# Moving weights and operands by bytes within their buffers: split weights 192 bytes on in place of 64, one block operand 112 bytes on

## The chip, the cores and the metric

The kernel runs on one core of one Trainium2 chip. The metric is the device time of one execution in microseconds. The kernel before takes 1206.85 us (median of three runs, 1206.4 to 1207.08).

## What is computed

A two-layer decoder trunk on 512 tokens of width 1024, all in float32: RMSNorm, a token mixer, a residual add, RMSNorm, a SwiGLU FFN, a residual add; then the second layer and a last RMSNorm. The first layer's mixer is dilated window attention in three groups of eight heads, the second layer's a causal pooling mixer.

```python
def reference(x, attn_norm, w_qkv, w_attn_out, pool_norm, w_pool_in, w_pool_group, pool_scale,
              ffn_norm, w_ffn_gate_up, w_ffn_down, final_norm):
    for i in range(DEPTH):
        j = i // N_MIXERS
        if i % N_MIXERS == 0:
            x = x + dilated_attention_mixer(rmsnorm(x, attn_norm[j]), w_qkv[j], w_attn_out[j])
        else:
            x = x + pooling_mixer(rmsnorm(x, pool_norm[j]), w_pool_in[j], w_pool_group[j], pool_scale[j])
        x = x + swiglu_ffn(rmsnorm(x, ffn_norm[i]), w_ffn_gate_up[i], w_ffn_down[i])
    return rmsnorm(x, final_norm)
```

## The kernel before

Tokens lie along the free axis (512 columns), channels on the 128 partitions. Every large product is made exactly enough in float32 by splitting each operand into a high part, rounded to the matmul's input type, and a low part, the rest: a product is then three matmuls, high x high, high x low and low x high. These three are lines 424, 425 and 426 in `mult`, lines 294, 295 and 297 in `Product.add`, and lines 595, 596 and 597 in `values12`.

*Two kinds of product.* `Product` takes a plain unit of weights (class `Plain`): an 8 x 8 block product with 512 columns streamed in each matmul. `mult` serves `seven` and `chained`, which make two blocks of output from seven products of half size (Strassen's scheme, as Winograd arranges it), each with 256 columns streamed. Their weights come in a `Pair`: blocks, sums, more sums and the last block, which `Pair.steps` lists and `take` splits. Attention uses `seven` for queries, keys and the first group's values; the FFN uses `chained` for gate/up and for some of the down products. `values12` makes the other values of attention with the roles swapped: there the weights are streamed and the token operand is loaded.

*Stages.* In the traced execution attention with `seven` runs from about 100 to 425 us, the first FFN to about 806 us, the pooling mixer to about 870 us, the second FFN after that, and the last rows of output from about 1180 us. An FFN is cut into parts by `PARTS`; a part whose third entry is true makes its down products by `chained` on the hidden units as blocks (`operands`, `operands_right`, `operands_left` place them under keys `d`). They run from about 655 to 694 us and from 1015 to 1055 us, and for the first layer also around 770 to 800 us. The last two of the eight output blocks of the second layer are computed in halves of 256 columns with plain weights (`end`, at the bottom of the kernel), so that the last norm can begin early.

*Where operands lie.* Three kinds of buffers matter.
- Split weights: the rings `w` (five buffers) and `half` (two). A buffer has room for a high and a low part and `LINE` = 64 elements (256 bytes) more; class `Held` places both parts `shift` elements on (an element is 4 bytes). `Plain` asks for no shift. `pairs` passes its `shift` to `Pair`: 16 elements by default, which attention's queries, keys and first values take, `APART` = 28 elements for the pairs of `values12`, and 0 for all of the FFN.
- Split token operands: two big tiles, `near` (11 places) and `far` (15 places), each with some room behind, handed out by `slot`. With `apart=True` an operand is placed `APART` = 28 elements (112 bytes) on; the FFN's block operands are, attention's are not.
- Two more places outside the big tiles, the loose ones (`slot11` and `slot12`), which `slot` gives when the big tiles have no place. They are tiles of their own and have no shift, whatever `apart` says.

All these buffers begin at 128 modulo 256 bytes in their partition, so the offsets that the code adds decide how operand and weights stand to each other modulo 256 bytes.

*Order.* Nothing is scheduled automatically: the engines take their instructions in the order in which the program issues them. Weights are loaded ahead by `pump`, which runs after each block of a product: it issues the next load as soon as its buffers are free and then the next split. A load of a `Pair` is three DMAs from SP's queue and one from POOL's, which adds to data in place (line 160). The program reserves `dynamic_dma_scratch_size` bytes of each partition for the descriptors of POOL's DMAs.

Of the kernel before, what the change touches and what calls it, by code (L numbers as in the profile page):

```python
# [15 lines left out]
P = 128  # L16
S = 512
D = 1024
KC = D // P
HEADS = 8  # L20
DFF = 2816
FC = DFF // P
# [22 lines left out]
BUFS = {"w": 5, "half": 2, "raw": 4, "rawhalf": 2}  # L45
COLS = {"w": D, "half": D // 2, "raw": D, "rawhalf": D // 2}
LINE = 64
APART = 28
NEAR = 11
OPEN = 2  # L50
# [4 lines left out]
def units_of(n):  # L55
    return (n,) if n <= KC else (n // 2, n - n // 2)
# [7 lines left out]
def trunk(ctx: ExitStack, tc: tile.TileContext, xT, norms, w_first, w_qk, w_qkp, w_v0, w_v0p, w_v12, w_out, w_pair, w_down, w_dblock, w_pin, w_pgrp,  # L64
          consts, ident_in, invcnt_in, outT, outR):
    nc = tc.nc
    cpool = ctx.enter_context(tc.tile_pool(name="cpool", bufs=1))
# [23 lines left out]
    def split(hi, lo, v):  # L91
        nc.scalar.activation(hi, v, AF.Copy)  # L92
        nc.vector.tensor_tensor(lo, v, hi.bitcast(F32), op=OP.subtract)  # L93
# [7 lines left out]
    class Held:  # L101


        def __init__(self, ring, shift=0):
            self.live = True
            n = COLS[ring]
            if ring in ("w", "half"):
                t = wpool.tile([P, 2 * n + LINE], F32R, tag=ring, name=ring, bufs=BUFS[ring])
                self.t = [t[:, shift + i * n:shift + (i + 1) * n] for i in range(2)]
            else:  # L110
                self.t = wpool.tile([P, n], F32, tag=ring, name=ring, bufs=BUFS[ring])
            rings[ring].append(self)
# [8 lines left out]
    class Plain:  # L121


        def __init__(self, *srcs):
            self.srcs, self.n, self.w = srcs, sum(src.shape[-1] for src in srcs), None
            loads.append((self, {"raw": 1}, self.load))
            steps.append((self, "w", self.split))

# [5 lines left out]
                o += src.shape[-1]  # L134

        def split(self):
            self.w = Held("w")
            split(*(t[:, :self.n] for t in self.w.t), self.raw.t[:, :self.n])
            self.raw.done()

    class Pair:
# [21 lines left out]
        def take(self, name, ring, raw):  # L163
            self.w[name] = w = Held(ring, self.shift)
            w.n = self.n
            split(*(t[:, :raw.shape[-1]] for t in w.t), raw)
# [20 lines left out]
    loads, steps, units = deque(), deque(), deque()  # L187
# [15 lines left out]
                return  # L203
            steps.popleft()[2]()

    def pairs(*srcs, shift=LINE // 4, back=False):

        these = [Pair(src, shift, back) for src in srcs]
        for parts in zip(*(p.steps() for p in these)):
            steps.extend(parts)  # L210
        units.append(these)

    def plain_gu(layer, j):
        src = w_pair[layer, j]
        units.extend([Plain(src[:, S:3 * S]), Plain(src[:, 3 * S:], src[:, :S])])

    def plain(*srcs):
        units.extend([Plain(src) for src in srcs])

    for h in range(HEADS):  # L220
        if h == 0:
            plain(*[w_qk[u] for u in range(len(QK) - NF)])
        for g in range(3):
            if h == 1 and g < NSOLO:
                plain(*[w_qk[len(QK) - NF + 2 * g + c] for c in range(2)])
            elif h:
                pairs(w_qkp[3 * h - 3 - NSOLO + g])
        if h == 0:
            plain(w_v0[0], w_v0[1])
        elif h % 2 == 0:  # L230
            pairs(w_v0p[h // 2 - 1])
        else:
            pairs(w_v12[h // 2, 0], w_v12[h // 2, 1], shift=APART)
    plain(*[w_out[m] for m in range(KC)])

    def ffn_plan(layer):
        j = 0
        for i, (first, end, block) in enumerate(PARTS[layer]):
            while j < min(end + block, FC):
                if j < NPLAIN:  # L240
                    plain_gu(layer, j)
                else:
                    pairs(w_pair[layer, j], shift=0, back=True)
                j += 1
            if block:
                for m in range(K2):
                    pairs(w_dblock[sum(p[2] for l in range(layer) for p in PARTS[l]) + sum(p[2] for p in PARTS[layer][:i]), m],
                          shift=0, back=True)
            else:
                for m in range(KC):  # L250
                    o = first * P
                    for n in units_of(end - first):
                        units.append(Plain(w_down[layer, m, :, o:o + n * P]))
                        o += n * P

    ffn_plan(0)
    plain(*[w_pin[m] for m in PIN_ORDER])
    ffn_plan(1)

    def weights():  # L260
# [5 lines left out]
    class Product:  # L266
# [16 lines left out]
        def add(self, ks, cols=slice(0, S), pos=None):  # L283
            for k in ks:
                if self.w:
                    w, c = self.w, k if pos is None else pos + k
                else:
                    held, c = self.where(k)
                    w = held.t
                    if c == self.sizes[len(self.tiles) - 1] - 1 and not self.keep:  # L290
                        held.done()
                s = slice(c * P, (c + 1) * P)
                mh, ml = self.ins(k)
                nc.tensor.matmul(self.p[:, cols], w[0][:, s], mh[:, cols], start=self.done == 0, stop=False)  # L294
                nc.tensor.matmul(self.p[:, cols], w[0][:, s], ml[:, cols], start=False, stop=False)  # L295
                self.done += 1
                nc.tensor.matmul(self.p[:, cols], w[1][:, s], mh[:, cols], start=False, stop=self.done == self.n)  # L297
            if not self.w:
                pump(2)
            return self  # L300
# [4 lines left out]
    def slot(name, dtype=F32R, apart=False, open=False, far=False):  # L305


        top, low = range(FIXED + SLOTS - 1, FIXED - 1, -1), range(FIXED, FIXED + SLOTS)
        near, loose = list(range(NEAR)), list(range(NEAR, FIXED))
        if "far" not in room:  # L310
            top = low = []
        if dtype == F32 or open:
            order = loose
        elif apart:
            order = [*top, *near[::-1], *loose]
        else:
            order = [*low, *near, *loose] if far else [*near, *low, *loose]
        i = next(i for i in order if i not in taken and (i in loose or taken.get(i + 1) is not False if apart else i in loose or not taken.get(i - 1)))
        if i in loose:
            taken[i] = None  # L320
            return i, cpool.tile([P, 2, S], dtype, tag=f"slot{i}", name=name, bufs=1)
        taken[i] = apart
        o = (i - FIXED * (i >= FIXED)) * 2 * S + APART * apart
        return i, room["far" if i >= FIXED else "near"][:, o:o + 2 * S].rearrange("p (e c) -> p e c", e=2)

    room["near"] = cpool.tile([P, NEAR * 2 * S + LINE], F32R, name="near")

# [10 lines left out]
    def product(layer):  # L338
        return Product(KC, stream(layer)).add(range(KC)).p
# [20 lines left out]
    def note(layer, k):  # L360

        if layer < 4:
            held[layer, k], t = slot("h", open=layer == 2 and k == KC - 1)
            scaled(layer, k, t[:, 0], t[:, 1])
        square(layer, k)
# [163 lines left out]
    class Temp:  # L529
        def __init__(self):  # L530
            self.i, t = slot("temp", F32)
            self.t = t.rearrange("p e c -> p (e c)")
# [30 lines left out]
    with tc.tile_pool(name="opool", bufs=1) as opool:  # L563
        early = opool.tile([P, HEADS, S], F32R, tag="o", name="early")
        with tc.tile_pool(name="apool", bufs=1) as apool:
# [253 lines left out]
            H, T, o = {}, {}, []  # L819
# [92 lines left out]
            for c in range(2):  # L912
                p = product(0)
# [57 lines left out]
            for m in range(KC):  # L971
                if lead:
                    f = lead.pop(0).add([last])
                else:
                    f = Product(HEADS, heads).add(range(HEADS))
# [6 lines left out]
    with tc.tile_pool(name="fpool", bufs=2) as fpool:  # L982

        room["far"] = fpool.tile([P, SLOTS * 2 * S + LINE // 2], F32R, tag="far", name="far", bufs=1)

# [284 lines left out]
        def end(i, half, js, f=None):  # L1270
            f = f or Product(HALF, hidden, keep=ends[i])
            return f.add(js, cols=halves[half])
# [39 lines left out]
        def total(half, sq):  # L1312
            t = ftile("total", H2)
            nc.vector.tensor_add(t, acc[4][:, halves[half]], sq)
            return t

        t = total(0, add(0, 0, end(0, 0, range(HALF))))
        sq = add(1, 0, end(1, 0, range(HALF)))
        f = end(0, 1, range(5))
        r = rstd([t, sq])  # L1320
        end(0, 1, range(5, HALF), f)
        t = total(1, add(0, 1, f))
        f = end(1, 1, range(1))
# [3 lines left out]
        f = end(1, 1, range(1, HALF), f)  # L1327
# [96 lines left out]
```

## Time and profile before

| | |
|---|---|
| median of three runs | 1206.85 us (1206.4 to 1207.08) |
| profiled execution, its own time | 1206.44 us |
| its span, first to last instruction | 1204.6 us |
| granted TensorE clock, mean | 0.998 |
| busy: PE, weight loads (PEld), DVE, ACT, POOL | 1193.7, 1117.6, 966.3, 658.0, 138.7 us |
| DMA | 183.65 MB, mean 152 GB/s |

PE is the matmul engine, PEld its weight loads, which overlap the matmuls. In the groups by line a row gives the line, engine, operation, tile written <- tiles read, shape and count, then busy time in us and the mean duration of one in ns, then the engine's idle time before them. Matmuls are pipelined: a clean one of 256 columns shows 275 ns, though the next begins some 113 ns after it. A longer duration goes with a later start of the next. In a table of stretches a row has start and end, length, busy time with the count of instructions, the granted clock, the share of time in which the DMA engines are busy, and GB/s.

### The profile page before, as it was taken

How to read it: one execution, taken by the hardware profiler on the slowest of the kernel's cores; microseconds unless marked ns; L12 is line 12 of the kernel's file. 1: busy time of each engine (PE TensorE's matmuls, PEld its weight loads, DVE VectorE, ACT ScalarE, POOL GpSimd, SP SyncE). 2: the span in 40 equal slices, each digit the busy share in tenths (PEclk: the TensorE clock that was granted, in tenths of full speed). 3: DMA queues.
4: the chain of work that ended last, by engine and by line, in shares of the span. 5: the costliest groups of instructions: out<-in, count | busy, mean ns of one | idle time of the engine just before them, and what ended most of it. 6: DMA issues, size and time to landing. Idle time of an engine off the chain costs nothing.

```text
span 1204.6 us, 24247 instructions
## 1 busy us (share of the span) xinstructions
PE 1193.7 (99%) x9720; PEld 1117.6 (93%) x9720; DVE 966.3 (80%) x1650; ACT 658.0 (55%) x1162; POOL 138.7 (12%) x131
## 2 busy tenths in 40 slices
PE   9999999999999999999999999999999999999997
PEld 7889999999999988888999999988788999999987
DVE  7888888878889854965898889989997898788633
ACT  6545554555556543542677567663443676566531
POOL 1111111111111100101111111000300111111000
PEclk9999999999999999999999999999999999999999
DMA  8346667666756532336677777644016677777322
GB/s 292 112 103 171 144 158 169 162 166 150 179 150 158 190 123 91 96 106 142 177 199 192 186 196 192 182 149 140 28 53 166 162 196 187 192 192 190 110 77 71
DMA packets 71152, 183.65 MB, mean 152 GB/s; under 512 B 7152, under 2 KB 8320, under 8 KB 71040
## 3 DMA queue, kind: packets, MB, share of 16 engines
q1 hardware_dynamic: 49824, 140.41, 35.7%
q0 software_dynamic: 21072, 41.43, 20.9%
q8 instruction: 76, 1.25, 0.4%
q14 instruction: 36, 0.29, 0.1%
q10 hardware_dynamic: 144, 0.26, 0.1%
HBM read 179.98 MB, written 2.10 MB: 151 GB/s over the span
## 4 chain that ended last, share of the span: by engine, by line
PE 91%; DVE 5%; issue 2%; ACT 1%; POOL 0%; DVEq 0%; POOLq 0%; DMA 0%; ACTq 0%
PE ps L424 17%; PE ps L425 17%; PE ps L426 17%; PE ps L294 9%; PE ps L295 9%; PE ps L297 9%; PE ps L595 2%; PE ps L597 2%; PE ps L596 2%; DVE w L93 1%; PE ps L807 1%; PE ps L679 1%; DVE s L1223 1%; PE ps L699 1%; PE ps L801 1%
## 5 line engine op out<-in xcount | busy, mean ns | idle before, releaser
L92 ACT ACTIVATE w<-raw 128x1024 fp32r<-128x1024 f32 (+3 forms) x303 | 309.8, 1028 | 258.3 <-PE ps L297 84.3
L93 DVE TENSOR_TENSOR w<-raw,w 128x1024 fp32r<-128x1024 f32 (+3 forms) x303 | 356.1, 1180 | 76.3 <-ACT w L92 72.3
L424 PE MATMUL ps<-far,w 128*128 128x256 f32 x860 | 236.7, 275 | 0.0
L425 PE MATMUL ps<-far,w 128*128 128x256 f32 x860 | 236.7, 275 | 0.0
L426 PE MATMUL ps<-far,w 128*128 128x256 f32 x860 | 236.6, 275 | 0.0
L425 PEld LDWEIGHTS ps<-far,w 128*128 128x128 f32 x860 | 161.5, 188 | 0.1
L424 PEld LDWEIGHTS ps<-far,w 128*128 128x128 f32 x860 | 161.5, 188 | 0.1
L426 PEld LDWEIGHTS ps<-far,w 128*128 128x128 f32 x860 | 161.4, 188 | 0.0
L424 PE MATMUL ps<-near,w 128*128 128x256 f32 x556 | 158.1, 284 | 1.5 <-ACT first L506 1.5
L425 PE MATMUL ps<-near,w 128*128 128x256 f32 x556 | 154.3, 278 | 0.0
L426 PE MATMUL ps<-near,w 128*128 128x256 f32 x556 | 154.3, 277 | 0.0
L295 PE MATMUL ps<-near,w 128*128 128x512 f32 (+1 forms) x364 | 137.7, 378 | 0.6 <-DVE near L357 0.6
L294 PE MATMUL ps<-near,w 128*128 128x512 f32 (+1 forms) x364 | 138.1, 380 | 0.0
L297 PE MATMUL ps<-near,w 128*128 128x512 f32 (+1 forms) x364 | 137.3, 378 | 0.0
L424 PEld LDWEIGHTS ps<-near,w 128*128 128x128 f32 x556 | 104.8, 188 | 2.5 <-ACT first L506 2.1
L425 PEld LDWEIGHTS ps<-near,w 128*128 128x128 f32 x556 | 104.6, 188 | 0.0
L426 PEld LDWEIGHTS ps<-near,w 128*128 128x128 f32 x556 | 104.5, 188 | 0.0
L160 POOL DMA_DIRECT2D raw<-w_pair x34 | 41.2, 1210 | 366.5 <-DMA raw<-w_pair 200.1
L295 PEld LDWEIGHTS ps<-near,w 128*128 128x128 f32 x364 | 68.5, 188 | 14.0 <-DVE near L357 1.7
L297 PEld LDWEIGHTS ps<-near,w 128*128 128x128 f32 x364 | 68.5, 188 | 12.8
L294 PEld LDWEIGHTS ps<-near,w 128*128 128x128 f32 x364 | 68.5, 188 | 12.5
L92 ACT ACTIVATE half<-rawhalf 128x512 fp32r<-128x512 f32 x75 | 47.2, 631 | 14.4 <-PE ps L426 12.3
(323 smaller groups left out, 2671.1 us busy)
## 6 DMA issues: line engine op xcount, KB each, us to landing
raw<-w_pair SPq DMA_DIRECT2D x78, 512.0 KB, 4.5
raw<-w_qkp SPq DMA_DIRECT2D x36, 512.0 KB, 4.2
raw<-w_pair POOLq DMA_DIRECT2D x34, 512.0 KB, 7.4
raw<-w_dblock SPq DMA_DIRECT2D x24, 512.0 KB, 4.1
raw<-w_v SPq DMA_DIRECT2D x18, 512.0 KB, 4.4
raw<-w_qkp POOLq DMA_DIRECT2D x18, 512.0 KB, 7.6
rawhalf<-w_pair SPq DMA_DIRECT2D x34, 256.0 KB, 5.1
raw<-w_dblock POOLq DMA_DIRECT2D x12, 512.0 KB, 7.5
```

Source lines behind the costliest of these rows:

```text
L92: nc.scalar.activation(hi, v, AF.Copy)
L93: nc.vector.tensor_tensor(lo, v, hi.bitcast(F32), op=OP.subtract)
L160: nc.gpsimd.dma_start(self.b.rearrange("p (a c) -> p a c", a=2), self.src[:, None, 3 * n:].to_broadcast([P, 2, n]), accum_op=OP.add)
L294: nc.tensor.matmul(self.p[:, cols], w[0][:, s], mh[:, cols], start=self.done == 0, stop=False)
L295: nc.tensor.matmul(self.p[:, cols], w[0][:, s], ml[:, cols], start=False, stop=False)
L297: nc.tensor.matmul(self.p[:, cols], w[1][:, s], mh[:, cols], start=False, stop=self.done == self.n)
L424: nc.tensor.matmul(dst, w.t[0][:, c], th, start=k == 0 and not on, stop=False, skip_group_check=on)
L425: nc.tensor.matmul(dst, w.t[0][:, c], tl, start=False, stop=False, skip_group_check=on)
L426: nc.tensor.matmul(dst, w.t[1][:, c], th, start=False, stop=k == n - 1, skip_group_check=on)
L595: nc.tensor.matmul(o, mh, wh, start=k == 0, stop=False)
L596: nc.tensor.matmul(o, mh, wl, start=False, stop=False)
L597: nc.tensor.matmul(o, ml, wh, start=False, stop=k == K2 - 1)
```

## The change

Only addresses change; what is computed, loaded and issued, and in which order, stays.
- The default shift of `pairs` goes from 16 to 48 elements, that is from 64 to 192 bytes. `values12` and the FFN pass their own and keep it.
- The plain weights of the last two output blocks of the second layer's last FFN part get a shift of 48 elements in place of 0.
- The two loose tiles become 256 bytes larger, and with `apart=True` their operand lies 28 elements (112 bytes) on, as in the big tiles.
- To make room, POOL's descriptor scratch goes from 4096 to 2048 bytes a partition. The tiles ahead of the loose ones move down by 2048 bytes and those behind by 1536, both multiples of 256.

```diff
+BEHIND = 48
...
-        def __init__(self, *srcs):
-            self.srcs, self.n, self.w = srcs, sum(src.shape[-1] for src in srcs), None
+        def __init__(self, *srcs, shift=0):
+            self.srcs, self.n, self.w, self.shift = srcs, sum(src.shape[-1] for src in srcs), None, shift
...
-            self.w = Held("w")
+            self.w = Held("w", self.shift)
...
-    def pairs(*srcs, shift=LINE // 4, back=False):
+    def pairs(*srcs, shift=BEHIND, back=False):
...
-                        units.append(Plain(w_down[layer, m, :, o:o + n * P]))
+                        units.append(Plain(w_down[layer, m, :, o:o + n * P],
+                                           shift=BEHIND * (layer == 1 and end == FC and m >= KC - 2)))
...
-            return i, cpool.tile([P, 2, S], dtype, tag=f"slot{i}", name=name, bufs=1)
+            t = cpool.tile([P, 2 * S + LINE], dtype, tag=f"slot{i}", name=name, bufs=1)
+            o = APART * apart
+            return i, t[:, o:o + 2 * S].rearrange("p (e c) -> p e c", e=2)
...
-    nc = bacc.Bacc("TRN2", target_bir_lowering=False, num_devices=1, dynamic_dma_scratch_size=4096)
+    nc = bacc.Bacc("TRN2", target_bir_lowering=False, num_devices=1, dynamic_dma_scratch_size=2048)
```

## The prediction

> **What bounds the kernel now.** I read the page first, then the groups by line with shapes kept apart, then busy time by stretch. The page's first lines and its chain of work:
> ```profile
> span 1204.6 us, 24247 instructions
> PE 1193.7 (99%) x9720; PEld 1117.6 (93%) x9720; DVE 966.3 (80%) x1650; ACT 658.0 (55%) x1162; POOL 138.7 (12%) x131
> PE 91%; DVE 5%; issue 2%; ACT 1%; POOL 0%; DVEq 0%; POOLq 0%; DMA 0%; ACTq 0%
> ```
> PE is busy 99% of the span and holds 91% of the chain that ended last. Nothing in the change adds, drops or moves an instruction: set side by side, both programs have the same instructions, operand shapes and waits on every engine. What differs is where buffers lie. So the time can only move through the price of one instruction, and on this kernel that means the price of one matmul.
>
> That price is not the same everywhere. These stretches hold only matmuls of 256 columns (start and end, length, busy time with the count in brackets, granted clock, DMA):
> ```profile
> 152.00:163.00 11.00, 11.00 (x94) 1.00 0.64 164
> 182.00:193.00 11.00, 11.00 (x99) 1.00 0.50 121
> 655.50:694.50 39.00, 39.00 (x338) 1.00 0.73 191
> 700.00:739.00 39.00, 39.00 (x347) 1.00 0.75 194
> 1015.70:1054.70 39.00, 39.00 (x338) 1.00 0.73 191
> 1060.00:1099.00 39.00, 39.00 (x347) 1.00 0.73 195
> 1181.00:1187.00 6.00, 6.00 (x52) 1.00 0.01 3
> ```
> The clock is full in all of them and PE never idles, yet 39 us take 347 matmuls in the gate/up stages and only 338 in the two stages just before them, and attention does 94 in one stretch of 11 us and 99 in another. A count takes in the two or three that overlap an edge, so the rates are 39/345, or 113 ns a matmul, and 6/50, or 120 ns, in the last row. The duration of one matmul follows the same steps. In the stage from 655.5 to 694.5 us:
> ```profile
> L425 PE MATMUL ps<-near,w 128*128 128x256 f32 x74 | 20.6, 278 | 0.0
> L424 PE MATMUL ps<-far,w 128*128 128x256 f32 x11 | 3.1, 282 | 0.0
> L426 PE MATMUL ps<-d,w 128*128 128x256 f32 x12 | 3.4, 281 | 0.0
> ```
> and over the whole run:
> ```profile
> L424 PE MATMUL ps<-far,w 128*128 128x256 f32 x860 | 236.7, 275 | 0.0
> L294 PE MATMUL ps<-near,w 128*128 128x256 f32 x40 | 11.5, 287 | 0.0
> L295 PE MATMUL ps<-near,w 128*128 128x256 f32 x40 | 11.3, 283 | 0.0
> L297 PE MATMUL ps<-near,w 128*128 128x256 f32 x40 | 11.3, 283 | 0.0
> ```
> 275 ns is the clean price. What sorts these rows is the byte offset between the streamed operand and the weights of the next matmul, which load meanwhile. Offsets are taken within 256 bytes, as the code sets them. `far` and the split operands of the FFN lie 112 bytes on and their weights at 0: weights 112 behind, 275 ns. In the last halves (lines 294 to 297) both lie at 0: 283 ns. The `d` tiles are block operands that found no place in the big tiles and so lie at 0 like their weights: 281 ns, and they spoil the `far` and `near` products that follow them, though those are 112 apart.
>
> **Attention.** Here the operands lie at 0 and the weights 64 on. By lines 424 to 426, from 100 to 425 us:
> ```profile
> L424 PE MATMUL ps<-near,w 128*128 128x256 f32 x336 | 96.7, 288 | 0.0
> L425 PE MATMUL ps<-near,w 128*128 128x256 f32 x336 | 93.4, 278 | 0.0
> L425 PE MATMUL ps<-tx,w 128*128 128x256 f32 x126 | 35.0, 277 | 0.0
> L425 PE MATMUL ps<-h,w 128*128 128x256 f32 x42 | 11.7, 277 | 0.0
> L425 PE MATMUL ps<-near,half 128*128 128x256 f32 x42 | 11.6, 277 | 0.0
> L425 PE MATMUL ps<-tx,half 128*128 128x256 f32 x42 | 11.6, 277 | 0.0
> ```
> The mean hides two prices. From 152 to 163 us, and then from 182 to 191.2 us, the same line reads:
> ```profile
> L425 PE MATMUL ps<-near,w 128*128 128x256 f32 x19 | 5.3, 281 | 0.0
> L425 PE MATMUL ps<-near,w 128*128 128x256 f32 x16 | 4.4, 276 | 0.0
> ```
> So with weights 64 bytes ahead a product runs either at 276 or at 281, for tens of matmuls on end; the mean of 277 to 278 says about a third run slow.
>
> **The change part by part.**
>
> *Block operand outside the big tiles, 112 on.* It gives the `d` tiles the offset of their neighbours, so these stages should run like those behind them: 347 matmuls where there were 338. Nine matmuls at 39/345 = 0.113 us are 1.0 us, in two stages: **2.0 us off**. Bounds: nothing, if `d` is not what starts the slow stretches, and 2.1 (9 or so, an edge more) from above. I take 2.0, since 275 is what 860 such matmuls show at that offset.
>
> *Last halves, weights 192 on.* 3 x 40 matmuls at 283 against 275 to 276: 120 x 7 to 8 ns, 0.84 to 0.96 us if the new offset is clean, nothing if it is as bad as 0. No row shows weights 192 on (64 behind). Equal offsets are the dearest seen, so I take **0.7 us off**.
>
> *Attention, weights 192 in place of 64.* (336 + 126 + 42 + 42 + 42) x 3 = 1764 matmuls. If all became clean at 276: 336 x 3 x 2 ns = 2.0 us, plus 252 x 3 x 1.3 ns = 1.0 us (277 rounds 35.0/126 and the like), so 3.0 us off, within 0.9 for the rounding of half a ns. If all ran at 281: 1764 x 3.3 ns = 5.8 us on. If all ran at the 283 of equal offsets: 1764 x 5.3 ns = 9.3 us on. The offset 64 behind has no row; it stands between 112 behind (275, settled) and 0 (283 throughout), and 64 ahead is mixed. I lean to the row for 112 behind, because there the dearer matmuls do not last. After a wait it does appear, as here from 775.9 to 777.1 us:
> ```profile
> L424 PE MATMUL ps<-near,w 128*128 128x256 f32 x3 | 0.9, 315 | 0.7 <-ACT first L506 0.7
> L426 PE MATMUL ps<-near,w 128*128 128x256 f32 x3 | 0.8, 281 | 0.0
> ```
> and the product after it is back at 275. Some ten matmuls at 5 ns over are 0.05 us a wait. Attention's waits show in line 424, the first of each triple; from 129 to 133.4 us one of them lifts the mean of four from 281 to 302:
> ```profile
> L424 PE MATMUL ps<-near,w 128*128 128x256 f32 x4 | 1.2, 302 | 0.0
> ```
> 4 x 21 = 84 ns a wait. Over attention line 424 stands 10 ns above line 425: 336 x 10 ns = 3.4 us, about 40 waits. 40 x 0.05 = 2.0 us would be left, so the gain lies between 1.0 and 3.0. I take **1.5 us off**, low in that span because the row is 48 bytes away.
>
> *Plain products* of 512 columns (attention's first head, output projection, gate/up of the first units) keep offset 0 and are untouched. `values12` keeps its 28 elements.
>
> *Smaller scratch, 2048 for 4096 bytes, and 256 bytes more for each of two tiles.* All tiles move by 2048 or 1536 bytes, multiples of 256, so no offset above shifts by it. The scratch serves the DMAs that POOL issues:
> ```profile
> raw<-w_pair POOLq DMA_DIRECT2D x34, 512.0 KB, 7.4
> x<-xT POOLq DMA_DIRECT2D x8, 256.0 KB, 6.7
> POOL raw L160 <- DMA raw<-w_pair: 200.1, 14, 51.9
> ```
> POOL waits for the data that it adds to, up to 51.9 us at once, and is busy 12%; its DMAs land 7 us after issue. I cost it at nothing; that cover fails only if the eight `xT` loads in a row and a pair's load exceed the smaller room, and then PE waits for weights that came a landing (7 us) late, once or twice.
>
> **Does the gain reach the end?** PE sets the end except in one stretch, where the chain goes through DVE, beginning
> ```profile
> 756.01 1.07 ACT w L92
> 757.10 0.69 DVE w L93
> 760.25 1.13 DVE w L93
> ```
> and lasting to about 871 us. It is entered from PE (before 756 the chain is lines 424 to 426), so work done earlier by PE lets it begin earlier. I let everything through.
>
> **Sum.** 2.0 + 0.7 + 1.5 = 4.2 us. The profiled execution took 1206.44 us with a span of 1204.6; the runs' median is 1206.85, 0.4 more. So the profile after should have a span near 1200.4, and the median **1202.6 us**.
>
> **A rule against it.** The rows above show PE slowed by the place of its own two operands. The Trainium skill, "SBUF — State Buffer", section "Who interferes with whom", gives PE two independent read ports, one for the streamed operand and one for weights, and says that PE and ACT never wait on anyone; by that, offsets would cost nothing and the time would stay 1206.85 (283 against 275 ns for the same shape at full clock disagrees).
>
> **Rivals.**
> 1. *64 behind is a bad place, for good (slower).* If the conflict reaches from 64 ahead through 0 to 64 behind, attention stays at the dearer price instead of leaving it. At 281 the sum is +5.8 - 2.0 - 0.2 = +3.6, 1210.5 us; at 283, +9.3 - 2.0 = +7.3, 1214.2. It turns slower by over 0.2% (2.4 us) once attention's mean passes 277.7 + (2.4 + 2.2)/1.764, about 280.3 ns. For it: equal offsets hurt always and 64 ahead a third of the time, so the zone is wide. Against: 112 behind settles. Chance 0.14.
> 2. *Attention stays as mixed as it is,* because 64 behind mirrors 64 ahead: only 2.0 + 0.4 go, 1204.4 us, on the border of 0.2%. Chance 0.2.
> 3. *Offsets do nothing;* the steps come from what else runs at that time: 1206.85. For it: DMA share and load differ between 152 and 182 us. Against: the last halves are slow at a DMA share of 0.01. Chance 0.08.
> 4. *The DVE stretch keeps what comes before it:* attention and the first block stage (2.5 us) are lost at 756 to 871 us and 1.7 stay, 1205.1 us. Against: it is entered from PE. Chance 0.06.
> 5. *The smaller scratch holds up POOL's DMAs,* one landing of 7 us late after heads: 1202.6 + 7 = 1209.6. Against: POOL's idle time. Chance 0.04.
>
> **The numbers.** Forecast 0.48. Faster by over 0.2%, about what a measurement of this kernel can tell from no change (below 1204.4): the forecast and half of rival 2, 0.58. Within 0.2%: the rest of 2, rivals 3 and 4, and the milder part of 1: 0.26. Slower: the rest of 1, and 5: 0.16. The range runs from 1201.0 (attention clean, 2.0 + 0.8 + 3.0) to 1208.6, which takes in rivals 2 to 4 and leaves out most of 1 and 5. The likeliest case alone spans 1201.0 to 1203.8.
>
> **What would show it.** The `d` rows at 275 and 347 matmuls in both block stages would confirm the first term; lines 294 to 297 at 275 to 276 the second; lines 425 and 426 in attention at 276 to 277 the third. Attention at 281 or more throughout makes the prediction wrong, as does a slow stretch in the block stages with `d` at 112, or new waits of PE for weights.

## The result, and the profile after

The change makes the kernel slower. Its median is 1209.13 us (15 runs, 1208.44 to 1209.62) against 1206.85 (15 runs, 1206.27 to 1207.19): a ratio of 1.0019, 95% interval 1.0011 to 1.0027, or 2.3 us. 1202.6 was forecast, with a range from 1201.0 to 1208.6. The profiled execution took 1208.44 us.

The page of the changed kernel, its first lines and its chain (line numbers are 2 to 4 higher than before):
```profile
span 1206.7 us, 24247 instructions
PE 1195.6 (99%) x9720; PEld 1119.8 (93%) x9720; DVE 967.0 (80%) x1650; ACT 658.1 (55%) x1162; POOL 139.9 (12%) x131
PE 91%; DVE 5%; issue 2%; ACT 1%; POOL 0%; DVEq 0%; POOLq 0%; DMA 0%; ACTq 0%
```
The span is 2.1 us longer, PE's busy time 1.9, and the chain is what it was. So it is still the price of single matmuls. The stretches again (start and end, length, busy time with count, clock, DMA): two of attention, the two block stages, the last halves:
```profile
152.40:163.40 11.00, 11.00 (x95) 1.00 0.67 167
182.00:193.00 11.00, 11.00 (x96) 1.00 0.50 118
658.90:697.90 39.00, 39.00 (x347) 1.00 0.74 196
1017.90:1056.90 39.00, 39.00 (x347) 1.00 0.74 197
1183.00:1189.00 6.00, 6.00 (x53) 1.00 0.01 3
```
Both block stages now do 347 matmuls in 39 us where they did 338: what was forecast there came exactly. The last halves do 53 where they did 52. But attention's second stretch, which did 99, does 96: its cheap matmuls are nearly gone. The groups, over the whole run for the `d` tiles and the halves, from 100 to 430 us for attention:
```profile
L430 PE MATMUL ps<-d,w 128*128 128x256 f32 x24 | 6.6, 275 | 0.0
L296 PE MATMUL ps<-near,w 128*128 128x256 f32 x40 | 11.4, 284 | 0.0
L297 PE MATMUL ps<-near,w 128*128 128x256 f32 x40 | 11.2, 279 | 0.0
L299 PE MATMUL ps<-near,w 128*128 128x256 f32 x40 | 11.2, 280 | 0.0
L429 PE MATMUL ps<-near,w 128*128 128x256 f32 x336 | 93.7, 279 | 0.0
```
`d` is at 275; the halves' second and third lines stand at 279 and 280 in place of 283, their first at 284 in place of 287; attention is at 279 in place of 277 to 278.

Durations of matmuls are modelled at their ends, so from here on I use the time from one matmul's start to the next one's. Clean matmuls of 256 columns begin 113 to 114 ns apart; I give every other mean as "ns over", which is what it has over 113, and call a matmul dear when it takes over 2 ns more than a clean one (113.3). Attention's other matmuls interrupt `mult`, which is entered again 39 times; at 36 of these entries the second matmul begins 200 to 230 ns after the first. Without these 36, 1689 matmuls of attention's `mult` are followed by another one, and their mean is 1.72 ns over before and 4.36 after: 2.9 us became 7.4, 4.5 us more. Following the same matmul through both traces gives the whole account: the changed kernel, 0.1 us ahead at the start of attention, is 4.4 us late after it, 3.4 after the first block stage, 2.3 after the second, and 2.0 at the last matmul.

PE's waits did not change: the longest group, for `first` on ACT, is three waits of 1.5 us together in both.

### The profile page after: what moved, and what is told of

It reads as the page before. It is cut to its first block, busy times and chain, and to the rows that moved or that the text cites. A ratio compares the mean times of both kernels' runs of the same rounds, so it can differ in the third digit from the quotient of the medians.

```text
span 1206.7 us, 24247 instructions
## 1 busy us (share of the span) xinstructions
PE 1195.6 (99%) x9720; PEld 1119.8 (93%) x9720; DVE 967.0 (80%) x1650; ACT 658.1 (55%) x1162; POOL 139.9 (12%) x131
## 4 chain that ended last, share of the span: by engine, by line
PE 91%; DVE 5%; issue 2%; ACT 1%; POOL 0%; DVEq 0%; POOLq 0%; DMA 0%; ACTq 0%
PE ps L428 17%; PE ps L430 17%; PE ps L429 17%; PE ps L296 9%; PE ps L297 9%; PE ps L299 9%; PE ps L599 2%; PE ps L601 2%; PE ps L600 2%; DVE w L94 1%; PE ps L811 1%; PE ps L683 1%; DVE s L1227 1%; PE ps L703 1%; PE ps L805 1%
```

## Experiments

Theory A at the outset: the byte distance between the streamed operand and the next weights, modulo 256, sets the price, and 64 behind is a bad distance. Rival B: what moved with the change (tiles by 2048 or 1536 bytes, the halved scratch) hurts attention.

**One part undone, one part alone.** Attention's weights back at 64, in the changed kernel:
```diff
-    def pairs(*srcs, shift=BEHIND, back=False):
+    def pairs(*srcs, shift=16, back=False):
```


> The changed kernel with one part undone: attention's split weights 64 bytes on again (shift 16); block operand, last halves and the smaller scratch stay. Theory A (the byte offset alone sets the price; 64 behind holds attention at the dear price): attention's 1764 matmuls are back at a mean of 277 to 278 ns, the 4.4 us that attention lost come back, and what stays is the block stages' 2.0 and the halves' 0.2: 1206.85 - 2.2 = 1204.7 us. Rival B (the moved tiles or the halved scratch cost the time in attention, not the offset): attention stays at 280 to 281 ns and the time near 1209.1.

And the kernel before with that part alone:
```diff
-    def pairs(*srcs, shift=LINE // 4, back=False):
+    def pairs(*srcs, shift=48, back=False):
```


> The kernel before with one part alone: attention's split weights 192 bytes on; tiles, scratch, block operand and halves as before. Theory A: attention goes to a mean of about 280 to 281 ns and loses 4.4 us, nothing else moves: 1211.2 us. Rival B (moved tiles or scratch): no change, 1206.85.

Measured: 1204.71 us with the part undone (10 runs; ratio to before 0.9983, interval 0.9974 to 0.9993), and 1211.43 with the part alone (4 runs; 1.0039, 1.0024 to 1.0054). Attention's row in the first and in the second:
```profile
L429 PE MATMUL ps<-near,w 128*128 128x256 f32 x336 | 93.4, 278 | 0.0
```
```profile
L425 PE MATMUL ps<-near,w 128*128 128x256 f32 x336 | 93.7, 279 | 0.0
```
From start to start the first is 1.72 ns over, as before, and the second 4.36, as after. The second has neither the smaller scratch nor the moved tiles: rival B is out. What is left in the first, 2.1 us against the 1206.85 of before, is the block operand's 2.0 and the halves' 0.2. It beats both kernels.

**Is it the distance?** The FFN's own distance, 112 behind, got by shifting the weights; and 112 ahead:
```diff
-    def pairs(*srcs, shift=BEHIND, back=False):
+    def pairs(*srcs, shift=36, back=False):
...
-                                           shift=BEHIND * (layer == 1 and end == FC and m >= KC - 2)))
+                                           shift=36 * (layer == 1 and end == FC and m >= KC - 2)))
```
(28 and 16 in the other kernel.)

> The changed kernel with attention's split weights and the last halves' weights 144 bytes on (shift 36), which is 112 behind, the FFN's own offset. Theory A with the prices of the FFN's rows (275 ns, some ten dearer matmuls after each wait): attention gains 1.0 to 2.5 us against the kernel before and the halves 0.7, so with the blocks' 2.0 the time is 1201.6 to 1203.2. Rival C (what counts is whether attention's operands lie at 0 at all, not the distance): attention stays at 280 to 281 as with 192 and the halves at 281 to 283, 1209 us.

> The changed kernel with attention's split weights 112 bytes on (112 ahead) and the last halves' weights 64 on (64 ahead). It tells whether ahead and behind mirror each other. Theory A': they do; 112 ahead is as 112 behind, clean at 275 to 276 but for some matmuls after a wait, and the halves at 64 ahead run at 281 or, in part, at 276: 1202 to 1203.5. Rival D: ahead is worse than behind, as weights that are late run into the stream; attention at 280 or more and 1208 or more.

Measured: 1213.05 us (4 runs; 1.0053, 1.0038 to 1.0068) and 1213.51 (4 runs; 1.0057, 1.0042 to 1.0072). Attention at 144 and at 112:
```profile
L429 PE MATMUL ps<-near,w 128*128 128x256 f32 x336 | 95.0, 283 | 0.0
```
```profile
L429 PE MATMUL ps<-near,w 128*128 128x256 f32 x336 | 95.1, 283 | 0.0
```
6.3 and 7.0 ns over, nearly as dear as equal offsets. Theory A with the FFN's prices falls at its own distance; so does the mirror. Rival C had the direction but not the size: it gave 280 to 281 ns and 1209 us, and 283 and 1213.05 came. Rival D's bounds, 280 or more and 1208 or more, hold, but nothing here tests its reason. The halves stand at 6.8 (144) and 4.3 (64). So either weights may not lie just anywhere, or it matters which of the two is shifted. Theory E: each operand's own place counts; weights want a 64-byte boundary, the streamed operand its 112.

**The FFN's arrangement in attention,** operands shifted and weights at 0:
```diff
-    def pairs(*srcs, shift=BEHIND, back=False):
+    def pairs(*srcs, shift=0, back=False):
...
+        apart = apart or dtype == F32R
         if "far" not in room:
...
-        return cpool.tile([P, S], dtype, tag=f"x{k}", name=name)
+        o = APART * (name == "tx")
+        return cpool.tile([P, S + LINE // 2], dtype, tag=f"x{k}", name=name)[:, o:o + S]
```
and no shift for the halves' weights.

> The changed kernel with the FFN's arrangement everywhere: all split token operands 112 bytes on (half of the tx tiles, whose room does not allow it, come to lie 16 bytes before a 256-byte boundary's half: 128 bytes from the others) and all weights of mult and of the last halves at 0. The difference between the two is the same as with weights 144 on, which ran at 280 to 283 ns. Theory E (not the difference decides, but where each operand itself lies: weights on a 64-byte boundary, the streamed operand 112 on): attention's mult and the last halves run at 275 to 276 ns but for some matmuls after a wait. Theory A (the difference decides): attention stays at 281 and more. values12 is changed with it (both its operands come to lie 112 on), so the whole time is no test: at worst its 672 matmuls cost 7 ns more, 4.7 us.

Measured: 1214.79 us (3 runs; 1.0063, 1.0040 to 1.0086), of which `values12` and the plain products explain a good part. By lines, attention's `near` and `tx`, `values12`, and the halves of 256 columns:
```profile
L431 PE MATMUL ps<-near,w 128*128 128x256 f32 x336 | 93.5, 278 | 0.0
L430 PE MATMUL ps<-tx,w 128*128 128x256 f32 x126 | 35.1, 279 | 0.0
L602 PE MATMUL ps<-w,near 128*128 128x256 f32 x111 | 31.2, 281 | 0.0
L298 PE MATMUL ps<-far,w 128*128 128x256 f32 x32 | 8.8, 276 | 0.0
```
The last halves are the clean test, as nothing stands between their matmuls: at the distance that cost 6.8 ns over with the weights moved, they are at 1.2 with the operand moved, and 276 ns. So the distance alone does not decide. In attention the operands that lie as in the FFN are at 2.9; between them stand `tx` tiles of which half lie 128 bytes further, and those, at 4.2, spoil their neighbours as the `d` tiles did. `values12`, where both operands now lie 112 on, went from 0.9 to 4.8 ns over.

**A sweep of the weights' place,** in the changed kernel, with another shift for the halves in each: 128 and 224, 32 and 96, 0 and 128, 80 and 48, 240 and 16, 176 and 208 bytes (the same two lines as above, shift 32 and 56, 8 and 24, and so on). One execution each.

> The changed kernel with attention's weights 128 bytes on and the last halves' 224 on. Theory E with 64-byte boundaries: 128 is as good as 64 or 192 (dear price 281, some share clean), 224 lies off a boundary and runs at 282 to 284. Theory A (distance): 128 is the farthest from 0 and the best of all, attention at 275 to 276; 224 is near 0 and as bad as 0, 283.

> The changed kernel with attention's weights 32 bytes on and the last halves' 96 on. Theory E with 64-byte boundaries: both lie off a boundary, 282 to 284 ns, attention like 144 (6 ns over). If 32-byte boundaries are enough: attention at 281 or less. Theory A (distance): 96 better than 32, between 64 and 112.

> The changed kernel with attention's weights at 0 and the last halves' 128 on. Both theories: attention at equal offsets runs at 283 ns as the last halves did, 1764 x 5.3 ns or 9 us more than before less the blocks' 2.0, 1213.5 us. The halves at 128: 281 or less by E, 275 to 276 by A.

> The changed kernel with attention's weights 80 bytes on and the last halves' 48 on. If clean places form a band around 64 ahead, 80 keeps some of it: attention below 3 ns over, 1204 to 1207 us. If only exact places serve (weights on a 64-byte boundary), attention stands at 5 ns and more over the clean start-to-start time, 1209 us and more; the halves stay between 4 and 7 over either way, as every shift of their weights has so far.

> The changed kernel with attention's weights 240 bytes on, 16 behind, and the last halves' 16 ahead. If the FFN's clean place comes of a 16-byte remainder between the operands (112 is 16 short of 128), 240 could be clean as well: attention under 1 ns over, 1203 us. If weights off a 64-byte boundary are always dear: 5 to 7 over, 1210 to 1214 us.

> The changed kernel with attention's weights 176 bytes on (80 behind) and the last halves' 208 on (48 behind): the neighbours of 192 on either side. If 192 lies at the edge of a clean band, one of the two shows a lower mean than 192's 4.4 over; if not, both stand at 4.5 to 7 over, 1209 to 1213 us.

Measured, with the runs above: attention's matmuls at each place of the weights, the mean time from start to start over 113 ns, and the share of them that pay over 2 ns more than clean, both counted from the start times in the traces; and the time of the kernel (the median where it ran more than once; the halves differ from row to row, which is worth at most 0.4 us).

| weights on, bytes | ns over, attention | share dear | kernel, us |
|---|---|---|---|
| 0 | 6.8 | 0.99 | 1214.29 |
| 32 | 5.3 | 0.96 | 1210.12 |
| 64 | 1.7 | 0.30 | 1204.71 |
| 80 | 5.7 | 0.98 | 1211.77 |
| 112 | 7.0 | 0.81 | 1213.51 |
| 128 | 5.6 | 0.80 | 1210.72 |
| 144 | 6.3 | 0.90 | 1213.05 |
| 176 | 5.2 | 0.83 | 1209.80 |
| 192 | 4.4 | 0.91 | 1209.13 |
| 240 | 5.5 | 0.88 | 1210.31 |

The halves, in the same measure: 6.9 at 0, 5.3 at 16 and at 48, 4.3 at 64, 4.6 at 96, 6.6 at 128, 6.8 at 144, 4.8 at 192, 4.2 at 208, 3.7 at 224. 64 is the one good place that was tried for attention; the farthest, 128, is not good, and a good band around 64, if there is one, reaches neither 32 nor 80. 64-byte boundaries do not suffice, as 0, 128 and 192 show. Of the forecasts, that for attention at 0 came out (1213.5 us, 1214.29 measured), and both theories missed the halves: 128 should have been at 281 ns or less and is at 283 to 286, and 224, bad by both, is the best place tried for the halves' weights. At 64, attention pays 1.72 ns over in `before` and in `att_back_to_64`, whose tiles lie 2048 or 1536 bytes lower: shifts by these multiples of 256 did not matter.

Does something else that runs at the time set the price? In the last halves of the kernel before, from 1181 to 1187 us, DVE is busy 1.54 us, ACT 1.31 and POOL not at all, at a DMA share of 0.01, and yet 99% of the halves' matmuls are dear.

**The FFN's weights 64 on,** its operands at 112, attention back at 64:
```diff
-                    pairs(w_pair[layer, j], shift=0, back=True)
+                    pairs(w_pair[layer, j], shift=16, back=True)
...
-                          shift=0, back=True)
+                          shift=16, back=True)
```


> The changed kernel with attention's weights back at 64, the last halves' at 224, and all the FFN's pair weights 64 bytes on in place of 0, their operands still 112 on: 48 behind in place of 112. Theory E in its wide form (weights on any 64-byte boundary, operand 112 on): the FFN stays at 275 ns, 1204.6 us. Narrow form (place of both within 256 bytes counts, each pair of places has its own price): the FFN's 3800 matmuls become dear by 2 to 7 ns, 1212 to 1231 us. Distance alone (theory A) would have 48 behind worse than 112 behind too.

Measured: 1221.85 us (one execution). A stage of gate/up, and the group that stood at 275 (the halves' weights are at 224 in this kernel):
```profile
704.00:743.00 39.00, 39.00 (x332) 1.00 0.70 182
```
```profile
L429 PE MATMUL ps<-far,w 128*128 128x256 f32 x860 | 241.8, 281 | 0.0
```
332 matmuls in place of 347; 5.3 ns over, every one of them dear. The wide form of theory E falls too; the narrow form stands: each pair of places that was tried has its own price, and neither the distance nor a boundary tells it. The place that is good for attention's weights is bad for the FFN's. It is the largest effect of the study, 17 us from 64 bytes.

**What makes 192 worse than 64.** In a dear product both pay the same: 117.8 ns from start to start, for tens of matmuls. The changed kernel has clean products too; here is a clean stretch, from 144.5 to 150.8 us, and a dear one, from 153 to 163 us:
```profile
L429 PE MATMUL ps<-near,w 128*128 128x256 f32 x11 | 3.0, 276 | 0.0
```
```profile
L429 PE MATMUL ps<-near,w 128*128 128x256 f32 x17 | 4.7, 279 | 0.0
```
What differs is the share of products that run dear. To see what decides it, a small matmul ahead of each product of `seven` interrupts PE:
```diff
+    product_of = mult
...
+        def mult(dst, *r):
+            nc.tensor.matmul(dst[:, :1], ident, ident[:, :1], start=True, stop=True)
+            product_of(dst, *r)
```


> The changed kernel with one small matmul (128x1, from the identity) ahead of each of the seven products of every pair of attention, 168 in all; it writes a column that the product then overwrites. It costs some 0.1 to 0.3 us each and is no improvement. Theory F (the entry decides, by the offset): nearly all products run dear, 118 ns, as at the natural entries, whatever ran before. Rival G (the price is carried over, and only what ran before decides): the share stays at 90%, but the products that follow a clean one stay clean for several products on end.

> The same with attention's weights 64 bytes on. Theory F: most products fall to the clean price, 113.3 ns, within a few matmuls of their entry, the ones that ran dear on end (such as those right after values12) too: share of dear matmuls at 29% or below. Rival G: the same stretches as before run dear, 29%, and the small matmuls change nothing.

Measured: 1238.28 and 1237.5 us (one execution each). Attention has 147 such products, not the 168 that were written. The small matmul, two records each, at 192:
```profile
L451 PE MATMUL ps<-ident 128*128 128x1 f32 x294 | 42.0, 212 | 0.0
```
Counted from the start times: at 192, 90 products run clean and 57 dear, 39% of the matmuls dear; at 64, 105 and 42, 30%. A product keeps the price at which it settles, within some five matmuls of its entry. So theory F fails for 192, which is not dear at nearly every entry. Rival G had the share wrong (90%), but the rest of its forecast came out: behind a clean product, several on end stay clean. What stands ahead of the small matmul tells more. For 39 of the 147 products it is other work of attention, for 108 only the product before:

| dear products | 192 | 64 |
|---|---|---|
| the kernel's own 39 entries, no small matmul | 35 of 39 | 12 of 39 |
| the same entries, small matmul added | 33 of 39 | 30 of 39 |
| small matmul alone, behind a clean product | 0 of 66 | 0 of 72 |
| small matmul alone, behind a dear product | 24 of 42 | 12 of 36 |

In these runs nothing turned dear behind the small matmul alone: every dear stretch began behind other work, and a small matmul could end it. Nor is it chance. In both runs the pattern repeats after 49 products, in 98 of 98 comparisons. In the kernels without small matmuls each of the 39 entries has the same price in `before` as in `att_back_to_64`, and the same in `after` as in `att_alone_192`. So what stands at an entry decides together with the offset: at the kernel's own entries 192 settles dear in 35 and 64 in 12, which is nearly the whole difference between them. It also tells why the last halves, with the weights at 64 and the operand at 0 as in attention, pay 4.3 where attention pays 1.7: of their three stretches two settle dear and one clean.

## Why the prediction was wrong

*Right:* that only the price of one matmul could move, that the place of operand and weights moves it (though the entry counts too), and that everything reaches the end. PE's waits are unchanged to 0.1 us, the DVE stretch at 756 us kept nothing (3.4 us late ahead of it and behind it), and the smaller scratch cost nothing (1204.71 with it).

*Right, and of the right size:* the block operand. 2.0 us were forecast, 347 matmuls a stage; 1.0 us came in each of the two stages, with `d` at 275.

*Right sign, wrong size:* the last halves. 0.7 us were forecast, 0.2 came: 4.8 ns over in place of 6.9. I took "equal offsets are the dearest" for "any other is nearly clean".

*Wrong:* attention, 1.5 us off forecast, 4.5 on measured. The step that failed is "I lean to the row for 112 behind, because there the dearer matmuls do not last". That row came from operands moved and weights at 0; I read its price as one of the distance, and put 64 behind on a line between 112 behind and 0. The runs show that no such line exists: at 112 behind by its weights, attention pays 6.3 ns over. The upper bound in the text, all at 281 for 5.8 us on, held the outcome; nine in ten ran dear. (What the text calls attention's waits, 84 ns each in line 424, are its entries: the profile shows no wait of PE between 100 and 425 us. The count, about 40, is right, but what an entry leaves behind in attention was taken from a real wait in the FFN, where the dearer matmuls end.) The rival that came true is the first, "64 behind is a bad place", though not for good: with the small matmuls, 192 runs clean in 90 of 147 products. Its sum, 1210.5, was 1.4 too high, mainly because it let all of attention run dear, each 3.3 ns above the mean, 5.8 us, where 2.6 ns, 4.5 us, came.

*Wrong in weight:* the chance of that rival. The row of the last halves and attention's own mean showed that places other than the FFN's were dear in part or always; there was one clean arrangement in the trace, and I let it speak for an untried one.

Against the rule that was weighed: the Trainium skill, "SBUF — State Buffer", section "Who interferes with whom", has PE and ACT never wait on anyone, and gives PE's two read ports as independent. By that the place of PE's own operands would cost nothing, and the runs disagree: moving the FFN's weights by 64 bytes took the same matmuls from 275 to 281 ns and the kernel from 1204.71 to 1221.85 us. That the two reads meet at a port is not shown by this.

*Open:* why a pair of places is dear or clean, and which part of the work ahead of an entry decides between the two prices. The records of the weight loads do not tell: a load takes 188 ns in a gate/up stage at 64 as it does at 0.

## What to carry to other kernels

When a kernel is bound by matmuls with new weights each time, compare the time from start to start of the same shape in different stages; differences of 4% at full clock may come from where operand and weights lie. Measure an offset for each arrangement and do not carry it over by its distance: weights 64 bytes on were the best place tried in one product and cost 17 us in another. Undo the parts of a change one by one, since two good parts and a bad one look like a small loss; here leaving out the attention part gives 1204.71 us, 2.1 us better than before.

## What the runs showed of the hardware that was not expected

- One shape of matmul at full clock has two lasting prices with the same offsets, 113.3 and 117.8 ns from start to start; it settles within some five matmuls of an interruption and stays until the next. Which of the two it takes repeats from run to run.
- Shifting the streamed operand and shifting the weights the other way are not the same: 1.2 against 6.8 ns over, for the last halves at one and the same distance modulo 256 bytes.
- The width counts too. In the FFN's plain products, matmuls of 512 columns bear equal offsets for nothing (226.9 ns from start to start, 967 of them before, twice 113.4), where 256 columns are dear. With the operand 112 on and weights at 0, which is clean for the FFN's 256 columns (0.4 ns over), they take 231.1 ns (1010, in the kernel that moved all operands).
